# A gated MLP on one Trainium2 core: the last column group's gate by seven block products, and a down-projection that begins in the middle

## The chip, the cores and the metric

The kernel runs as one program on one core of a Trainium2 chip. The core has a matrix engine (TensorE; PE in the profile, its weight loads PEld), a vector engine (VectorE, DVE), a scalar engine (ScalarE, ACT), GpSimd (POOL) and a sync engine (SyncE, SP), which here only issues DMA transfers. Matmuls read SBUF and write PSUM banks of 128 x 512 numbers. The metric is the device time of one execution in microseconds.

## The reference, cut to what matters

Two layers of a decoder trunk work on 512 tokens of 1024 features: layer 0 has attention and a short convolution as its mixer, layer 1 a gated linear attention. Behind each mixer stands the gated MLP that the change touches, and behind that a small gated embedding:

```python
def _conv_ffn(h, w_up, conv_w, conv_b, w_down):
    u = _causal_depthwise_conv(h @ w_up, conv_w) + conv_b
    gate, up = jnp.split(u, 2, axis=-1)
    return (jax.nn.gelu(gate, approximate=False) * up) @ w_down

# in each layer i:
    x = x + _conv_ffn(_rms_norm(x, ffn_norm[i]), ffn_w_up[i], ffn_conv_w[i], ffn_conv_b[i], ffn_w_down[i])
```

`w_up` is 1024 x 5632: 2816 gate columns and 2816 value columns. `w_down` is 2816 x 1024. The convolution is causal, of width 3 along the tokens, with own weights for every column.

## The kernel before

Activations are kept with features on the 128 partitions and tokens along the row, so a tile is 128 features x 512 tokens. Everything is float32, done as three matmuls: each operand is split into a high part (ScalarE, rounded to the matmul's format) and a low part (VectorE, the rest), and a product is high x high, high x low and low x high (`mm3`, L153 to L160; `split`, L97). Weights are loaded 1024 x 256 numbers at a time into one of two `raw` buffers (8 KB a partition, 1 MB in all) and cut into high and low pieces `wh` and `wl` (`cut`, L119 to L139), of which three of each fit, a piece being 128 x 1024.

The MLP (`ffn`, L871) goes over its 2816 = 11 x 256 gate columns in 11 groups d = 0 to 10. A group makes two gate column tiles and two value column tiles, applies the three taps to each (`taps`, L883: one ScalarE pass and two VectorE passes), a Gelu to the gates, and multiplies gate and value (L1018). The product is two activations, numbers f = 2d and 2d + 1; there are 22. Groups come in two kinds:

- Plain groups (the `else` branch at L988): each of the four column tiles is 8 x 3 matmuls, 128 x 128 weights by 512 tokens. Weights are asked for under `high_priority(offset=300)`.
- Seven-product groups, `SEVEN = (4, 10)`, so d = 4 to 9 (L970): the gate's 1024 x 256 weights and the 512 tokens are taken as 2 x 2 blocks, and their product is formed from seven block products in place of eight, after the scheme of Strassen and Winograd (`seven`, L827). A block product is 4 x 3 matmuls of 256 tokens. VectorE forms the weights' sums for it (`seven_forms`, L813), and the tokens' sums are made once (`sums`, L771; list `forms`). The group's values stay plain, 48 matmuls of 512 tokens. The order of TensorE is written out by hand here (`manual_schedule(engines={ET.PE})`): the first steps of group d + 1 (18 + 12 + 6 matmuls, `begin`, L957) stand at the end of group d, and `prepare(d + 1)` (L950) loads and cuts its weights.

Buffers tie the parts together. The tag `four` has seven tiles of 128 x 4 x 512: five hold finished products (`kept`, four activations each), and the others take split activations, two activations with both parts in a tile. The tags `b0` and `b1` have eight tiles each: they hold the tokens' sums (`forms`) as long as seven-product groups run, and then split activations, one in a pair. The tag `zt` has two, so a group's gate and value tiles follow those of the group before.

When the last seven-product group (d = 9) is traced, activations 0 to 7 are split into `b` pairs (L1021); after the loop 8 to 21 are split into `four` tiles (L1026). The down-projection (`project`, L350) takes two of the eight output column tiles at a time, and for these three blocks of inputs: activations 0 to 7, 8 to 15 and 16 to 21, with a load and a cut for each. A block is 2 x 8 x 3 = 48 matmuls of 512 tokens (the last 36).

Other than where it is written out by hand, the order of each engine's list is set when the program is built, by a planner that takes the instructions in the order of the code as their priority, moves an instruction ahead by the given number of places under `high_priority`, and lets one start when its inputs and a free buffer are there. On the chip each engine then works its list in that order.

```python
                    with tc.high_priority(offset=300):
                        wg = self.weights(wu[:, :, gates(d)], ND, 256)
                        wv = self.weights(wu[:, :, values(d)], ND, 256)
```

Of the kernel before, what the change touches and what calls it, by code (L numbers as in the profile page):

```python
# [18 lines left out]
P = 128  # L19
# [3 lines left out]
ND = D // P  # L23
DFF = 2816
NF = DFF // P
# [3 lines left out]
ET = mybir.EngineType  # L29
LEVELS = (64, 32, 16, 8, 4, 2, 1)  # L30
CW = 512
SEVEN = (4, 10)
TWO_PI = 2.0 * np.pi
PI_SAFE = 3.1415925

# [22 lines left out]
class Kernel:  # L58
# [288 lines left out]
        nc.scalar.copy(R, pr)  # L347
        return R

    def project(self, load, ks, n_out, done):  # L350

        nk = len(ks)
        for m2 in range(0, n_out, 2):
            pss = [self.ps(), self.ps()]
            for k0 in range(0, nk, 8):
                kn = min(8, nk - k0)
                raw = self.raw(kn, 2 * P)
                load(raw, k0, slice(m2 * P, (m2 + 2) * P))
                w = self.cut(raw, "b")
                for c in range(2):  # L360
                    for k in range(kn):
                        self.mm3(
                            pss[c], w(k, c * P, (c + 1) * P), ks[k0 + k],
                            start=k0 + k == 0, stop=k0 + k == nk - 1,
                        )
            for c in range(2):
                done(m2 + c, pss[c])
# [503 lines left out]
    def ffn(self, i, next_gain):  # L871
        nc, a, tc = self.nc, self.a, self.tc
# [2 lines left out]
        wu = a["ffn_w_up"][i].rearrange("(k p) n -> p k n", p=P)  # L875
        w0, w1, w2, bb = self.fcv
        with tc.tile_pool(name=f"ffn{i}", bufs=1) as fp:
            forms, kept, acts = [], [], []

            def both():  # L880
                return fp.tile([P, 2, S], F32, tag="zt", name=self.nm("zt"), bufs=2)

            def taps(y, ps, f, more=None, normed=True):  # L883
                z = ps
                if more is not None:
                    z = fp.tile([P, S + 2], F32, tag="z", name=self.nm("z"), bufs=3)[:, :S]
                    h2 = lambda x: x.rearrange("p (u t) -> p u t", u=2)
                    nc.vector.tensor_tensor(
                        h2(z), h2(ps), more.unsqueeze(1).to_broadcast([P, 2, S // 2]), ALU.add
                    )  # L890
                elif not normed:
                    z = fp.tile([P, S + 2], F32, tag="z", name=self.nm("z"), bufs=3)[:, :S]
                    nc.vector.tensor_tensor(z, ps, R, ALU.mult)
                nc.scalar.activation(y, z, AF.Identity, scale=w2[:, f : f + 1], bias=bb[:, f : f + 1])  # L894
                for tap, w in ((1, w1), (2, w0)):
                    nc.vector.scalar_tensor_tensor(  # L896
                        out=y[:, tap:], in0=z[:, : S - tap], scalar=w[:, f : f + 1], in1=y[:, tap:],
                        op0=ALU.mult, op1=ALU.add,
                    )

            def columns(w, c, bank):
                ps = bank()
                for k in range(ND):
                    self.mm3(ps, w(k, c * P, (c + 1) * P), xg[k], start=k == 0, stop=k == ND - 1)
                return ps
# [10 lines left out]
            def place(d):  # L916

                if d == NF // 2 - 1:
                    return None
                if d % 2 == 0:  # L920
                    kept.append(self.four(fp, F32))
                return kept[d // 2][:, 2 * (d % 2) : 2 * (d % 2) + 2]

            def split_pair(x):
                four = self.four(fp)
                self.split((four[:, :2], four[:, 2:]), x)
                acts.extend([(four[:, u], four[:, 2 + u]) for u in range(2)])

            def at(f):
                return kept[f // 4][:, f % 4]  # L930

            def gates(d):
                return slice(256 * d, 256 * d + 256)

            def values(d):
                return slice(DFF + 256 * d, DFF + 256 * d + 256)

            def normed(scratch):

                out = []  # L940
                for m in range(ND):
                    out.append(self.pair(self.fp, "a0", "a1"))
                    self.split(out[m], scratch[m // 2][:, m % 2])
                return out

            def value(w, ps, k0, k1):
                for k in range(k0, k1):
                    self.mm3(ps, w(k, 0, P), xg[k], start=k == 0, stop=k == ND - 1)

            def prepare(d):  # L950

                rg, rv = loaded(d)
                w1 = column(rv, 1)
                ws = self.seven_forms(rg)
                return self.seven(rg, ws, xg, forms), w1, column(rv, 0)

            def begin(d, steps, w):  # L957

                ps = self.pa()
                value(w, ps, 0, 6)  # L960
                next(steps)
                value(w, ps, 6, ND)
                return lambda y: taps(y[:, 1], ps, NF + 2 * d + 1)

            first, last = SEVEN
            scratch = [self.four(fp, F32) for _ in range(ND // 2)]
            late = None
            for d in range(NF // 2):
                g, y = both(), both()
                if first <= d < last:  # L970
                    with tc.manual_schedule(engines={ET.PE}):
                        next(steps)
                        V0 = self.pa()
                        value(w0c, V0, 0, ND // 2)
                        next(steps)
                        value(w0c, V0, ND // 2, ND)
                        X, Y, more = next(steps)
                        mine = late

                        if d + 1 < last:  # L980
                            steps, w1c, w0c = prepare(d + 1)
                            late = begin(d + 1, steps, w1c)
                        mine(y)
                        taps(y[:, 0], V0, NF + 2 * d)
                        taps(g[:, 0], X, 2 * d)
                        taps(g[:, 1], Y, 2 * d + 1, more)
                        nc.scalar.activation(g, g, AF.Gelu)
                else:  # L988
# [4 lines that stand above are left out]
                    todo = []  # L993
                    for c in range(2):
                        pss = [columns(w, c, self.ps) for w in (wg, wv)]
                        if R is None:
                            R = self.spread()

                        def finish(c=c, pss=pss):
                            taps(g[:, c], pss[0], 2 * d + c, None, d > first)  # L1000
                            nc.scalar.activation(g[:, c], g[:, c], AF.Gelu)
                            taps(y[:, c], pss[1], NF + 2 * d + c, None, d > first)

                        if d == first - 1:
                            todo.append(finish)
                        else:
                            finish()
                    if d == first - 1:
                        xg = normed(scratch)
                        with tc.manual_schedule(engines={ET.PE}):  # L1010
                            steps, w1c, w0c = prepare(first)
                            late = begin(first, steps, w1c)
                        for f in todo:
                            f()
                u = place(d)
                if u is None:
                    u = y
                nc.vector.tensor_tensor(u, g, y, ALU.mult)  # L1018
                for j in {0: (0, 1), 1: (2, 3)}.get(d, ()):
                    forms.append(self.sums(j, gain, R, scratch[j]))  # L1020
                if d == last - 1:  # L1021
                    for f in range(8):
                        hl = self.pair(self.fp, "b0", "b1")
                        self.split(hl, at(f))
                        acts.append(hl)
            for d in range(4, NF // 2):  # L1026
                split_pair(y if d == NF // 2 - 1 else kept[d // 2][:, 2 * (d % 2) : 2 * (d % 2) + 2])
            self.begin_norm(("a0", "a1"))
            done = self.residual(next_gain)
            if i == 1:  # L1030
# [12 lines left out]
                    nc.vector.tensor_tensor(self.xT[m], self.xT[m], ps, ALU.add)  # L1043
                    self.blocks(m, next_gain, half)

            self.project(self.rows(a["ffn_w_down"][i]), acts, ND, done)
            if i == 0:
                self.end_norm()
            else:
# [704 lines left out]
```

## Time and profile before

| | us |
|---|---|
| median of 3 runs (1239.39 to 1239.8) | 1239.51 |
| the profiled execution | 1240.1 |
| its span, first to last instruction | 1238.3 |
| TensorE busy | 1227.8 |
| VectorE busy | 847.8 |
| ScalarE busy | 604.6 |
| GpSimd busy | 43.6 |

The profile is of one execution, whose own time is 1.8 us longer than the span of its instructions and 0.6 us above the median. A row of a group of instructions reads: line, engine, operation, output<-inputs with shapes, count | busy time, mean duration in ns | idle time of the engine before them and what ended it. In a table of stretches each row gives a stretch in microseconds from the span's start, its length, and the busy time of each engine with its instruction count, then the granted clock of TensorE (1.00 is full), the DMA share and the GB/s. In order of time a row gives start, duration, engine, line, operation, output<-inputs, shapes, count and, in brackets, the idle time before it. Matmuls are pipelined, so the pace of a series is read from its starts, not its durations.

### The profile page before, as it was taken

To read this page: it belongs to the slowest core of one execution; us is meant where nothing else is said; L and a number is where in the kernel's file an instruction comes from. 1 tells how busy PE (TensorE), PEld (TensorE's weight loads), DVE (VectorE), ACT (ScalarE), POOL (GpSimd) and SP (SyncE) were. 2 spreads that over 40 slices of the span, in tenths; PEclk is the share of its full clock that TensorE was granted. 3 is DMA by queue.
4 is the path that set the end of the run, shared out by engine and by line. 5 is a ranking of instruction groups with operands and counts; after the bars stand their busy time and mean duration, and the time that the engine had idled before them with its cause. 6 is when DMAs were issued, how large, how long until landed. Compare 5 with 4: busy or idle time off the path is not lost.

```text
span 1238.3 us, 16087 instructions
## 1 busy us (share of the span) xinstructions
PE 1227.8 (99%) x6416; PEld 1036.6 (84%) x6416; DVE 847.8 (68%) x1323; ACT 604.6 (49%) x963; POOL 43.6 (4%) x64
## 2 busy tenths in 40 slices
PE   9999999999999999999999999999999999999998
PEld 8877788889899888888987888888889998888887
DVE  6886556987778833346679875549977779544495
ACT  7466333555557522234563554435455558333374
POOL 2500000000000000000100000000000000000000
PEclk9999999999999999999999999999999999999999
DMA  7221332323233332223322222332332324222411
GB/s 215 86 88 51 88 103 69 102 69 124 81 109 111 109 99 94 94 80 99 111 91 68 69 69 68 102 98 83 101 108 71 129 77 137 94 94 94 152 44 69
DMA packets 111007, 117.50 MB, mean 95 GB/s; under 512 B 2728, under 2 KB 106210, under 8 KB 110932
## 3 DMA queue, kind: packets, MB, share of 16 engines
q1 hardware_dynamic: 109568, 115.35, 28.7%
q8 instruction: 50, 0.82, 0.3%
q0 software_dynamic: 560, 0.42, 0.3%
q10 hardware_dynamic: 804, 0.70, 0.2%
q14 instruction: 25, 0.20, 0.1%
HBM read 114.37 MB, written 2.10 MB: 94 GB/s over the span
## 4 chain that ended last, share of the span: by engine, by line
PE 88%; DVE 7%; ACT 2%; issue 2%; POOL 1%; DMA 0%; ACTq 0%; DVEq 0%; POOLq 0%
PE ps L158 19%; PE ps L159 19%; PE ps L160 19%; PE pa L159 4%; PE pa L158 4%; PE pa L160 4%; PE ps L844 2%; PE ps L843 2%; PE ps L842 2%; DVE wl L139 1%; PE ps L1168 1%; PE ps L1166 1%; PE ps L1167 1%; PE pa L844 1%; PE pa L843 1%
## 5 line engine op out<-in xcount | busy, mean ns | idle before, releaser
L138 ACT ACTIVATE wh<-raw 128x1024 fp32r<-128x1024 f32 (+4 forms) x188 | 188.4, 1004 | 324.6 <-PE ps L159 272.7
L139 DVE TENSOR_TENSOR wl<-raw,wh 128x1024 fp32r<-128x1024 f32 (+4 forms) x188 | 216.8, 1155 | 179.8 <-ACT wh L138 179.5
L158 PE MATMUL ps<-a,wh 128*128 128x512 f32 x480 | 187.6, 391 | 0.0
L159 PE MATMUL ps<-a,wh 128*128 128x512 f32 x480 | 187.2, 390 | 0.0
L160 PE MATMUL ps<-a,wl 128*128 128x512 f32 x480 | 186.9, 389 | 0.0
L158 PE MATMUL ps<-b,wh 128*128 128x512 f32 x320 | 126.0, 395 | 0.6 <-ACT b L102 0.5
L160 PE MATMUL ps<-b,wl 128*128 128x512 f32 x320 | 125.7, 393 | 0.0
L159 PE MATMUL ps<-b,wh 128*128 128x512 f32 x320 | 124.9, 391 | 0.0
L158 PEld LDWEIGHTS ps<-a,wh 128*128 128x128 f32 x480 | 90.2, 188 | 18.9 <-issue 0.7
L160 PEld LDWEIGHTS ps<-a,wl 128*128 128x128 f32 x480 | 90.1, 188 | 18.9
L159 PEld LDWEIGHTS ps<-a,wh 128*128 128x128 f32 x480 | 90.2, 188 | 18.7 <-issue 0.3
L158 PE MATMUL ps<-four,wh 128*128 128x512 f32 x224 | 87.1, 389 | 0.0
L159 PE MATMUL ps<-four,wh 128*128 128x512 f32 x224 | 87.1, 389 | 0.0
L160 PE MATMUL ps<-four,wl 128*128 128x512 f32 x224 | 87.1, 389 | 0.0
L158 PE MATMUL pa<-a,wh 128*128 128x512 f32 x192 | 75.3, 392 | 0.0
L159 PE MATMUL pa<-a,wh 128*128 128x512 f32 x192 | 75.3, 392 | 0.0
L160 PE MATMUL pa<-a,wl 128*128 128x512 f32 x192 | 74.7, 389 | 0.0
L158 PEld LDWEIGHTS ps<-b,wh 128*128 128x128 f32 x320 | 60.0, 188 | 14.2 <-ACT b L102 1.3
L159 PEld LDWEIGHTS ps<-b,wh 128*128 128x128 f32 x320 | 60.1, 188 | 12.5
L160 PEld LDWEIGHTS ps<-b,wl 128*128 128x128 f32 x320 | 60.1, 188 | 12.5
L896 DVE SCALAR_TENSOR_TENSOR zt<-z,vfa,zt 128x511 f32<-128x511 f32 (+1 forms) x88 | 64.0, 745 | 5.3 <-ACT zt L894 5.0
L807 ACT ACTIVATE wh<-raw 128x1024 fp32r<-128x1024 f32 x36 | 38.0, 1057 | 37.0 <-DVE raw L820 20.1
(423 smaller groups left out, 2509.3 us busy)
## 6 DMA issues: line engine op xcount, KB each, us to landing
raw<-in_ffn_w_up_dram SPq DMA_DIRECT2D x44, 1024.0 KB, 5.0
raw<-in_ffn_w_down_dram SPq DMA_DIRECT2D x16, 1024.0 KB, 5.0
raw<-in_hy_w_in_dram SPq DMA_DIRECT2D x8, 1024.0 KB, 5.1
raw<-in_gla_w_in_dram SPq DMA_DIRECT2D x8, 1024.0 KB, 5.2
raw<-in_ffn_w_down_dram SPq DMA_DIRECT2D x8, 768.0 KB, 4.5
raw<-in_ple_w_gate_dram SPq DMA_DIRECT2D x6, 1024.0 KB, 5.0
raw<-in_gla_w_out_dram SPq DMA_DIRECT2D x4, 1024.0 KB, 5.1
raw<-in_gla_w_in_dram SPq DMA_DIRECT2D x4, 672.0 KB, 4.1
```

Of the source, the lines that this page charges most:

```text
L138: nc.scalar.activation(hv, v, AF.Copy)
L139: nc.vector.tensor_tensor(lv, v, hv.bitcast(F32), ALU.subtract)
L158: mm(out, lh, rh, start=start, stop=False)
L159: mm(out, lh, rl, start=False, stop=False)
L160: mm(out, ll, rh, start=False, stop=stop)
L807: nc.scalar.activation(h, src, AF.Copy)
L842: mm(out, wh, xh, start=first and j == 0, stop=False, **kw)
L843: mm(out, wh, xl, start=False, stop=False, **kw)
L844: mm(out, wl, xh, start=False, stop=j == ND // 2 - 1, **kw)
L896: nc.vector.scalar_tensor_tensor(out=y[:, tap:], in0=z[:, : S - tap], scalar=w[:, f : f + 1], in1=y[:, tap:], op0=ALU.mult, op1=ALU.add,)
L1166: mm(o, lh, rh, start=first and j == 0, stop=False, **kw)
L1167: mm(o, lh, rl, start=False, stop=False, **kw)
```

## The change

The last group, d = 10, becomes a seven-product group as well: `SEVEN = (4, 11)`. It is the last of that kind, so nothing is prepared behind its products; in that place the code now has `split_acts()`, which splits the finished activations 0 to 19 in a new order: 8 to 13 into `four` tiles, 0 to 3 into `b` pairs, 14 and 15, then 4 to 7 and 16 to 19. The split of 0 to 7 behind d = 9 and the loop behind all groups go; 20 and 21 are split when d = 10 is done. The list of activations is filled by number, not by appending.

`project` gets an argument `first`. For the first pair of output columns, the MLP's down-projection takes the block of activations 8 to 15 first, then 0 to 7, then 16 to 21, and its three loads and cuts are traced under `high_priority(offset=300)`. The later column pairs keep the old order. All other calls of `project`, and the later pairs, trace their loads under an offset of zero. The first and last matmul of an accumulation are marked by the new order of the blocks.

```diff
-SEVEN = (4, 10)
+SEVEN = (4, 11)
...
-    def project(self, load, ks, n_out, done):
+    def project(self, load, ks, n_out, done, first=()):
...
-            for k0 in range(0, nk, 8):
+            lead = [k0 for k0 in first if m2 == 0]
+            k0s = lead + [k0 for k0 in range(0, nk, 8) if k0 not in lead]
+            for k0 in k0s:
                 kn = min(8, nk - k0)
-                raw = self.raw(kn, 2 * P)
-                load(raw, k0, slice(m2 * P, (m2 + 2) * P))
-                w = self.cut(raw, "b")
+                with self.tc.high_priority(offset=300 if lead else 0):
+                    raw = self.raw(kn, 2 * P)
+                    load(raw, k0, slice(m2 * P, (m2 + 2) * P))
+                    w = self.cut(raw, "b")
                 for c in range(2):
                     for k in range(kn):
                         self.mm3(
                             pss[c], w(k, c * P, (c + 1) * P), ks[k0 + k],
-                            start=k0 + k == 0, stop=k0 + k == nk - 1,
+                            start=k0 == k0s[0] and k == 0, stop=k0 == k0s[-1] and k == kn - 1,
                         )
...
-            forms, kept, acts = [], [], []
+            forms, kept, acts = [], [], [None] * NF
...
-            def split_pair(x):
+            def split_pair(f, x=None):
+                if x is None:
+                    x = kept[f // 4][:, f % 4 : f % 4 + 2]
                 four = self.four(fp)
                 self.split((four[:, :2], four[:, 2:]), x)
-                acts.extend([(four[:, u], four[:, 2 + u]) for u in range(2)])
-
-            def at(f):
-                return kept[f // 4][:, f % 4]
+                acts[f : f + 2] = [(four[:, u], four[:, 2 + u]) for u in range(2)]
+
+            def split_kept(t):
+                for f in range(4 * t, 4 * t + 4):
+                    acts[f] = self.pair(self.fp, "b0", "b1")
+                    self.split(acts[f], kept[t][:, f % 4])
+
+            def split_acts():
+                for f in (8, 10, 12):
+                    split_pair(f)
+                split_kept(0)
+                split_pair(14)
+                split_kept(1)
+                for f in (16, 18):
+                    split_pair(f)
...
                         if d + 1 < last:
                             steps, w1c, w0c = prepare(d + 1)
                             late = begin(d + 1, steps, w1c)
+                        else:
+                            split_acts()
                         mine(y)
...
-                if d == last - 1:
-                    for f in range(8):
-                        hl = self.pair(self.fp, "b0", "b1")
-                        self.split(hl, at(f))
-                        acts.append(hl)
-            for d in range(4, NF // 2):
-                split_pair(y if d == NF // 2 - 1 else kept[d // 2][:, 2 * (d % 2) : 2 * (d % 2) + 2])
+            split_pair(NF - 2, y)
...
-            self.project(self.rows(a["ffn_w_down"][i]), acts, ND, done)
+            self.project(self.rows(a["ffn_w_down"][i]), acts, ND, done, first=(8,))
```

## The prediction

> **What bounds the kernel now.** I read the page first, then the waits of TensorE, then a table of stretches around the place of the change, then single instructions in order of time. The page:
>
> ```profile
> span 1238.3 us, 16087 instructions
> PE 1227.8 (99%) x6416; PEld 1036.6 (84%) x6416; DVE 847.8 (68%) x1323; ACT 604.6 (49%) x963; POOL 43.6 (4%) x64
> PEclk9999999999999999999999999999999999999999
> ...
> PE 88%; DVE 7%; ACT 2%; issue 2%; POOL 1%; DMA 0%; ACTq 0%; DVEq 0%; POOLq 0%
> ...
> raw<-in_ffn_w_up_dram SPq DMA_DIRECT2D x44, 1024.0 KB, 5.0
> ```
>
> See three things. TensorE is busy for 99% of the span at full granted clock, the chain that ended last is 88% TensorE, and a weight block lands 5.0 us after its issue. The busy share alone doesn't prove that matmuls follow each other without a hole, so the stretches come next: in each layer the last seven-product group (d = 9), the plain last group (d = 10), and the first two rows of the down-projection.
>
> ```profile
> core 0: us, PE busy (x) PEld busy (x) DVE busy (x) ACT busy (x) POOL busy (x), PEclk, DMA share, GB/s
> 378.03:399.06 21.03, 21.03 (x134) 19.07 (x133) 19.83 (x26) 16.36 (x24) 0.00 (x0) 1.00 0.31 101
> 399.06:420.85 21.79, 21.79 (x98) 18.04 (x97) 21.53 (x27) 14.49 (x20) 0.00 (x0) 1.00 0.30 97
> 420.85:450.77 29.92, 29.92 (x133) 24.77 (x132) 12.34 (x13) 8.67 (x10) 0.00 (x0) 1.00 0.31 101
> 1016.74:1037.78 21.04, 21.04 (x134) 19.08 (x133) 19.82 (x26) 16.37 (x24) 0.00 (x0) 1.00 0.31 100
> 1037.78:1059.57 21.79, 21.79 (x98) 18.03 (x97) 21.53 (x27) 14.48 (x20) 0.00 (x0) 1.00 0.30 97
> ```
>
> The columns are the stretch, its length, and each engine's busy time and instructions. TensorE is busy through all of each stretch (the count takes in two matmuls that overlap its edge: 132 and 96 by the code). So here the time is the sum of the paces of matmuls, and any hole would be new. VectorE is nearly as full as TensorE in the plain group (21.53 of 21.79 us) and has room only behind it (12.34 of 29.92 us).
>
> **The change, part by part.** *Fewer matmul columns.* The pace is read from starts, since matmuls overlap:
>
> ```profile
> 267.65 0.39 PE L159 MATMUL ps<-a,wh 128*128 128x512 f32 x1
> ...
> 276.72 0.39 PE L160 MATMUL pa<-a,wl 128*128 128x512 f32 x1
> 276.94 0.28 PE L842 MATMUL pa<-a,wh 128*128 128x256 f32 x1
> ...
> 278.25 0.28 PE L844 MATMUL pa<-a,wl 128*128 128x256 f32 x1
> ```
>
> From the first to the 41st of the wide ones: 9.07 / 40 = 0.227 us each. From the first to the 12th of the narrow ones: 1.31 / 11 = 0.119 us. A plain gate is 2 columns x 8 k x 3 = 48 wide matmuls, 10.88 us; seven products are 7 x 4 x 3 = 84 narrow ones, 10.00 us. That would be 0.88 us; the whole groups in the table differ by less, 21.79 - 21.04 = 0.75 us, because wide matmuls that follow narrow ones run a little slower. I take 0.75, since it holds all of that; two layers give **-1.50 us**. The bounds of this term are -1.50 and -1.76.
>
> The Trainium skill, "TensorE: Matmul & The Clock Gate", section "Wait — 56ns, not 53.3ns?", gives the pace as columns over 2.4 GHz and about 2.5 ns for each matmul. An estimate by it is 48 x 215.8 - 84 x 109.2 = 1.19 us a layer, -2.4 us in all. The rows above have some 13 ns over the columns' time on either width, five times that, and the 36 additional matmuls of a layer pay it; the trace decides.
>
> *What the seven form adds on VectorE and ScalarE.* Durations of the pieces:
>
> ```profile
> L139 DVE TENSOR_TENSOR wl<-raw,wh 128x1024 fp32r<-128x1024 f32 x152 | 185.6, 1223 | 114.5 <-ACT wh L138 114.1
> L896 DVE SCALAR_TENSOR_TENSOR zt<-z,vfa,zt 128x511 f32<-128x511 f32 x44 | 32.4, 746 | 5.0 <-ACT zt L894 5.0
> L1018 DVE TENSOR_TENSOR four<-zt,zt 128x1024 f32<-128x1024 f32 x20 | 24.4, 1220 | 0.1
> L103 DVE TENSOR_TENSOR b<-four,b 128x512 fp32r<-128x512 f32 x32 | 21.4, 684 | 0.0
> L103 DVE TENSOR_TENSOR four<-four,four 128x1024 fp32r<-128x1024 f32 x12 | 14.4, 1216 | 0.0
> L102 ACT ACTIVATE four<-four 128x1024 fp32r<-128x1024 f32 x12 | 12.4, 1052 | 2.2 <-DVE four L103 2.2
> L807 ACT ACTIVATE t<-raw 128x512 fp32r<-128x512 f32 x12 | 7.6, 637 | 0.2 <-DVE raw L822 0.2
> 386.60 0.37 ACT L858 COPY more<-pa 128x256 f32<-128x256 f32 x1 [0.54 <-PE pa L844]
> ```
>
> A plain group cuts four weight pieces, 4 x 1.22 = 4.9 us of VectorE. A seven group cuts five and a half-size one, subtracts four half-size blocks and adds one partial sum: 5 x 1.22 + 6 x 0.68 = 10.2 us (all of the six are 512 elements wide, as the b split is). So 5.3 us more for VectorE, and about 1.05 + 0.64 + 5 x 0.37 = 3.5 us for ScalarE (a cut, a half-size one, five half-bank copies). Its cover is the down-projection's first stretch, where VectorE is free for 29.92 - 12.34 = 17.6 us; on the path it costs nothing as long as the splits meet their two dates, worked out below.
>
> *The date of the first activations.* The down-projection now starts on activations 8 to 15. The old d = 9 group is the model for the new d = 10 group, since it too prepares no seven-product successor; moved on by one period of 21.04 us, its rows give the new times:
>
> ```profile
> 387.34 3.34 SPq L112 DMA_DIRECT2D raw<-in_ffn_w_up_dram  x2
> 390.20 1.22 DVE L1018 TENSOR_TENSOR four<-zt,zt 128x1024 f32<-128x1024 f32 x1
> 391.33 1.29 DVE L103 TENSOR_TENSOR b<-four,b 128x512 fp32r<-128x512 f32 x2
> 392.55 0.75 DVE L896 SCALAR_TENSOR_TENSOR zt<-pa,vfa,zt 128x511 f32<-128x511 f32 x1
> 393.21 0.68 DVE L103 TENSOR_TENSOR b<-four,b 128x512 fp32r<-128x512 f32 x1
> 393.81 0.74 DVE L896 SCALAR_TENSOR_TENSOR zt<-pa,vfa,zt 128x510 f32<-128x510 f32 x1
> 394.47 0.68 DVE L103 TENSOR_TENSOR b<-four,b 128x512 fp32r<-128x512 f32 x1
> 395.07 1.22 DVE L139 TENSOR_TENSOR wl<-raw,wh 128x1024 fp32r<-128x1024 f32 x1
> 396.20 2.35 DVE L103 TENSOR_TENSOR four<-four,four 128x1024 fp32r<-128x1024 f32 x2
> 398.48 1.22 DVE L139 TENSOR_TENSOR wl<-raw,wh 128x1024 fp32r<-128x1024 f32 x1
> ```
>
> The old d = 9 group ends where the table's second stretch begins, at 399.07; before that VectorE had already split four activations into b pairs and two pairs into fours, and cut the first two weight pieces. The new one ends at 420.1. Its d = 9 product (L1018) starts at 390.20 + 21.04 = 411.2. From there the list is that product 1.22, four fours (8 to 15) 4 x 1.22, four b pairs (0 to 3, which free the buffer for 14 and 15) 4 x 0.68, and the two weight cuts 2.44: 11.3 us, done at 422.5. Activation 14 is read by the 19th matmul of the down-projection, 420.1 + 18 x 0.227 = 424.2. That leaves 1.7 us. If the two taps of the late value column (2 x 0.75) stay ahead, as they were in d = 9, 0.2 us are left; against that, two of the seven fours buffers are free from the start, so 8 to 11 need not wait for 411.2. I take no stall. The bounds are nothing and 4.6 us a layer, worked out with the rivals.
>
> *The date of the last activations.* After 422.5 VectorE has four b pairs (4 to 7) 2.7, two fours (16 to 19) 2.4, eight taps 8 x 0.75 with one sum 0.7, the product 1.2, the split of 20 and 21 1.2, and four weight cuts 4 x 1.22 at most: 19.1 us, done at 441.6. The third block (activations 16 to 21) starts two blocks of 48 wide matmuls after 420.1, at 441.9, and reads activation 20 after 12 more, at 444.6. The cover is 3.0 us; each microsecond beyond it would be paid twice, once a layer.
>
> *Loads and weights.* The rows of SP: the plain weights were asked for at 387.34, 11.7 us ahead of their first matmul, and the first piece was cut at 395.07 + 1.22 = 396.3, 2.8 us ahead. The down-projection's first three blocks now get the same lead of 300 places, the numbers of loads stay (two for d = 10, three for the first columns), and they use the same two raw buffers. SP only issues loads, and d = 10's own pair now goes one period earlier, as d = 9's did without a hole. Cost nothing; bound without that cover 5.0 + 1.05 + 1.22 = 7.3 us a layer.
>
> *The rest.* Block order and the start and stop flags leave the 144 matmuls of a column pair as they are. The other projections get a lead of zero places; no row can show that this moves nothing, so I bound it by the longest wait of TensorE in the second mixer, which a shuffled order might repeat or take away:
>
> ```profile
> PE pa L1434 <- DVE F L1432: 1.5, 2, 1.0
> ```
>
> That is up to 1.0 us either way; I take zero, since that part of the program is untouched.
>
> Sum: the profiled execution took 1240.1 us (span 1238.3 and 1.8 around it) and should become 1240.1 - 1.5 = 1238.6. The median of the runs shown, 1239.51, lies 0.6 below it, so I predict 1239.5 - 1.5 = **1238.0 us**.
>
> **The rivals.** *First activations late* (the one that ends slower). Place: the first block of the down-projection. If VectorE began the splits only after the last product, act 8 would be ready 1.05 + 1.22 = 2.3 us after it and act 14 after 1.05 + 4 x 1.22 + 4 x 0.68 = 8.7 us, against a date of 4.1: 4.6 us a layer, 2 x 4.6 - 1.5 = +7.7, 1247 us. From 2.0 us a layer on (act 14 later than 6.1 us after the last product) it makes the kernel slower by over 0.2%. For it: a VectorE that is busy for 19.83 + 21.53 = 41.4 of 42.8 us. Against it: the splits at 391.33 and 396.20 ran inside a seven group. VectorE works its list in order, so a tap that waits for a bank would hold the splits behind it; the Trainium skill's same page, in its table of specifications, calls that queue strict FIFO, which no row here contradicts.
>
> *A short stall.* The same place or act 20, by 0.3 to 2.0 us a layer: 1238.6 to 1242.0, within 0.2%, about what a measurement of this kernel can tell from no change (2.5 us). For it: margins of 0.2 to 3.0 us.
>
> *A down-projection load takes a raw buffer ahead of d = 10's own weights.* Then TensorE waits a whole load and cut, 7.3 us a layer, 2 x 7.3 - 1.5 = +13.1, 1253 us. The 300 places reach back beyond the point where d = 10 is prepared. Against it: the plain weights had the same lead, and their load at 387.34 came a period after this row:
>
> ```profile
> 366.30 3.33 SPq L910 DMA_DIRECT2D raw<-in_ffn_w_up_dram  x2
> ```
>
> *The matmuls save something else.* If a matmul cost its columns alone, the 48 x 512 - 84 x 256 = 3072 columns fewer would be worth (0.227 - 0.119) / 256 = 0.42 ns each, 1.3 us a layer: 1236.9. If the narrow ones ate the gain, so that the change doesn't do what it says, 1239.5. The 0.75 us of whole groups speaks against both. The Trainium skill's rule for the pace, weighed above, stands near the first.
>
> **How the numbers follow.** No hole, 1238.0 (its own range 1237.0 to 1239.0: the 1.0 us of the mixers either way): 0.66. Short stall: 0.12. First activations late: 0.12. Load late: 0.05. Matmuls at their columns' cost: 0.02; no gain of the matmuls: 0.02; an unseen wait that goes, with over 2.5 us: 0.01. The range of 1237.0 to 1242.0 holds the first two and the sixth, 0.80. Faster by over 0.2%: 0.03; within: 0.80; slower: 0.17.
>
> **What would show it.** In the trace after: 168 more narrow matmuls and 96 fewer wide ones; a last group of 21.04 us in both layers; the first matmul of the down-projection on a four, 0.12 us behind the last narrow one; no wait of TensorE between the first seven group and the end of the down-projection. A wait of L158 on L103 (four) at its 1st, 7th, 13th or 19th matmul would show the first rival, one on L139 the third, one in the third block late last activations. The prediction is wrong if any hole over 2.0 us a layer stands there.

## The result and the profile after

The changed kernel takes 1237.99 us (median of 22 runs), the kernel before beside it 1239.83 (22 runs): a ratio of 0.9986 with a 95% interval of 0.9979 to 0.9992. That is 1.84 us less, and by the interval between 1.0 and 2.6 us less. One of the 22 runs of the changed kernel took 4132.6 us, for a reason that no profile here shows; the ratio and its interval leave it out. The profiled execution after took 1237.57 us, with a span of 1235.8.

The page of the kernel after, the lines that answer to those shown of before:

```profile
span 1235.8 us, 16256 instructions
PE 1225.1 (99%) x6488; PEld 1037.8 (84%) x6488; DVE 857.8 (69%) x1337; ACT 611.8 (50%) x975; POOL 44.2 (4%) x64
...
PEclk9999999999999999999999999999999999999999
...
PE 88%; DVE 7%; ACT 2%; issue 2%; POOL 1%; DMA 0%; SPq 0%; DVEq 0%; ACTq 0%; POOLq 0%
```

TensorE has 72 instructions more: 168 narrow matmuls more and 96 wide ones fewer. VectorE has 10.0 us more work and ScalarE 7.2, which is 5.0 and 3.6 a layer, and the chain that ended last is TensorE to the same 88%. So more work was done on two engines and a little less on the one that bounds the kernel.

The table of stretches of the kernel after (columns as in the prediction): in layer 0 the group d = 9, the group d = 10 and the down-projection's first stretch, then d = 10 of layer 1.

```profile
377.27:398.31 21.04, 21.04 (x135) 19.08 (x133) 19.38 (x24) 14.16 (x19) 0.00 (x0) 1.00 0.31 101
398.31:419.35 21.04, 21.04 (x135) 19.08 (x133) 19.69 (x26) 15.56 (x24) 0.00 (x0) 1.00 0.31 100
419.35:449.27 29.92, 29.92 (x134) 24.78 (x133) 19.44 (x23) 13.28 (x16) 0.00 (x0) 1.00 0.31 101
...
1035.94:1056.98 21.04, 21.04 (x134) 19.08 (x133) 19.57 (x26) 15.56 (x24) 0.00 (x0) 1.00 0.31 101
```

The last group is now 21.04 us long instead of 21.79, TensorE is busy through all of it, and VectorE's work in the down-projection's first stretch went from 12.34 to 19.44 us without lengthening that stretch by a hundredth.

Spans of single executions also differ where nothing was changed, so I measure every kernel below between the same two matmuls of a layer: the first one of the MLP's norm (on `ones` and `acc`) and the last one of the down-projection that reads `wh`. TensorE in order of time, first before, then after; the 615.14 and 613.35 rows are one matmul of the second mixer.

```profile
188.00 0.26 PE L324 MATMUL pa<-ones,acc 128*128 128x1 f32 x1
...
540.09 0.39 PE L159 MATMUL ps<-four,wh 128*128 128x512 f32 x1
...
615.14 0.51 PE L158 MATMUL ps<-b,wh 128*128 128x512 f32 x1 [0.17 <-ACT vt L1329]
...
826.69 0.26 PE L324 MATMUL pa<-ones,acc 128*128 128x1 f32 x1
...
1178.80 0.39 PE L159 MATMUL ps<-four,wh 128*128 128x512 f32 x1
```

```profile
187.24 0.26 PE L324 MATMUL pa<-ones,acc 128*128 128x1 f32 x1
...
419.23 0.28 PE L848 MATMUL ps<-a,wl 128*128 128x256 f32 x1
419.35 0.40 PE L158 MATMUL ps<-four,wh 128*128 128x512 f32 x1
...
423.46 0.39 PE L158 MATMUL ps<-four,wh 128*128 128x512 f32 x1
...
443.86 0.39 PE L158 MATMUL ps<-four,wh 128*128 128x512 f32 x1
...
538.60 0.39 PE L159 MATMUL ps<-four,wh 128*128 128x512 f32 x1
...
613.35 0.51 PE L158 MATMUL ps<-b,wh 128*128 128x512 f32 x1
...
824.88 0.26 PE L324 MATMUL pa<-ones,acc 128*128 128x1 f32 x1
...
1176.23 0.39 PE L159 MATMUL ps<-four,wh 128*128 128x512 f32 x1
```

Before: 540.09 - 188.00 = 352.09 and 1178.80 - 826.69 = 352.11. After: 351.36 and 351.35. The two MLPs are shorter by 0.73 and 0.76, together 1.49 us. The spans differ by 2.5, and most of the rest, 0.76 us, lies ahead of the first MLP (188.00 against 187.24), where both kernels issue the same instructions in the same order. So of the 1.84 us between the medians 1.49 are found in the changed part, and the other 0.35, which the interval of 1.0 to 2.6 doesn't tell from zero, I attribute to nothing. Among the kernels below, what lies outside the two stretches varies by some 1.5 us from one profiled execution to another, so I take stretches from the profile and totals from medians.

### The profile page after: what moved, and what is told of

Its sections match the earlier page's. It is cut to its first block, busy times and chain, and to the rows that moved or that the text cites. A ratio compares the mean times of both kernels' runs of the same rounds, so it can differ in the third digit from the quotient of the medians.

```text
span 1235.8 us, 16256 instructions
## 1 busy us (share of the span) xinstructions
PE 1225.1 (99%) x6488; PEld 1037.8 (84%) x6488; DVE 857.8 (69%) x1337; ACT 611.8 (50%) x975; POOL 44.2 (4%) x64
## 4 chain that ended last, share of the span: by engine, by line
PE 88%; DVE 7%; ACT 2%; issue 2%; POOL 1%; DMA 0%; SPq 0%; DVEq 0%; ACTq 0%; POOLq 0%
PE ps L158 18%; PE ps L159 18%; PE ps L160 18%; PE pa L159 5%; PE pa L158 5%; PE pa L160 5%; PE ps L848 3%; PE ps L847 3%; PE ps L846 3%; DVE wl L139 1%; PE pa L848 1%; PE pa L847 1%; PE pa L846 1%; PE ps L1181 1%; PE ps L1179 1%
## 5 line engine op out<-in xcount | busy, mean ns | idle before, releaser
L138 ACT ACTIVATE wh<-raw 128x1024 fp32r<-128x1024 f32 (+4 forms) x184 | 184.3, 1003 | 312.3 <-PE ps L159 258.5
L139 DVE TENSOR_TENSOR wl<-raw,wh 128x1024 fp32r<-128x1024 f32 (+4 forms) x184 | 212.0, 1153 | 166.3 <-ACT wh L138 165.9
L158 PE MATMUL ps<-a,wh 128*128 128x512 f32 x416 | 162.7, 391 | 0.0
L159 PE MATMUL ps<-a,wh 128*128 128x512 f32 x416 | 162.3, 390 | 0.0
L160 PE MATMUL ps<-a,wl 128*128 128x512 f32 x416 | 162.0, 390 | 0.0
L158 PEld LDWEIGHTS ps<-a,wh 128*128 128x128 f32 x416 | 78.1, 188 | 16.6 <-issue 0.7
L159 PEld LDWEIGHTS ps<-a,wh 128*128 128x128 f32 x416 | 78.2, 188 | 16.3 <-issue 0.3
L160 PEld LDWEIGHTS ps<-a,wl 128*128 128x128 f32 x416 | 78.1, 188 | 16.2
L158 PE MATMUL pa<-a,wh 128*128 128x512 f32 x224 | 87.8, 392 | 0.0
L159 PE MATMUL pa<-a,wh 128*128 128x512 f32 x224 | 87.8, 392 | 0.0
L160 PE MATMUL pa<-a,wl 128*128 128x512 f32 x224 | 87.1, 389 | 0.0
L900 DVE SCALAR_TENSOR_TENSOR zt<-z,vfa,zt 128x511 f32<-128x511 f32 (+1 forms) x92 | 66.9, 744 | 5.9 <-ACT zt L898 5.4
L811 ACT ACTIVATE wh<-raw 128x1024 fp32r<-128x1024 f32 x42 | 44.4, 1057 | 41.1 <-DVE raw L824 22.1
```

The source lines that it names most:

```text
L138: nc.scalar.activation(hv, v, AF.Copy)
L139: nc.vector.tensor_tensor(lv, v, hv.bitcast(F32), ALU.subtract)
L158: mm(out, lh, rh, start=start, stop=False)
L159: mm(out, lh, rl, start=False, stop=False)
L160: mm(out, ll, rh, start=False, stop=stop)
L811: nc.scalar.activation(h, src, AF.Copy)
```

## The experiments

My theory was the prediction's: seven products in place of eight are worth 0.75 us of TensorE in each group and layer, and everything else in the change only has to arrive on time. The rivals were that some of the gain comes from the new order of the splits and blocks or from the lead of the loads, that the splits are close to their date, or that the matmul term is another size. "Stretches" are the two differences of layer 0 and 1 against before, as above. Times are compared with runs of the kernel before on the same chip (medians 1239.77, 1239.91 and 1239.73 in the three series).

**Which part gives the gain: the seven products alone.** The kernel before with one constant changed; splits, blocks and lead stay the old ones.

```diff
-SEVEN = (4, 10)
+SEVEN = (4, 11)
```

> Seven products for the last group with nothing else: the down-projection starts on activations 0 to 7 without a lead, and four of their b pairs come free only when the last product has read the sums. The matmul account with ample cover: 1.5 us under before. The rival, that the new order and lead are what keeps TensorE fed: a hole of 2 to 5 us a layer ahead of the down-projection, so 2.5 to 8.5 us over before.

Measured: 1237.80 us (1237.21 to 1237.99), ratio 0.9984 (0.9975 to 0.9993); stretches -0.74 and -0.74. The table of stretches of this kernel, the last group of both layers:

```profile
398.78:419.82 21.04, 21.04 (x134) 19.08 (x133) 19.75 (x26) 15.52 (x24) 0.00 (x0) 1.00 0.31 100
1036.29:1057.33 21.04, 21.04 (x134) 19.08 (x133) 19.91 (x26) 15.52 (x24) 0.00 (x0) 1.00 0.32 101
```

No hole in either, and the same 21.04 us. The constant gives the whole gain; the new order and the lead add nothing that can be measured.

**The change without the lead.** The kernel after, its down-projection loads traced like all others.

```diff
-                with self.tc.high_priority(offset=300 if lead else 0):
+                with self.tc.high_priority(offset=0):
```

> The changed kernel without the lead of 300 places for the first three blocks; block order and splits as changed. If the planner would place loads and cuts early anyhow, because buffers are free: like the changed kernel, 1.5 us under before. If the lead matters: the first cut comes behind the splits and taps, a hole of 1 to 5 us a layer, so 0.5 to 8.5 us over before.

Measured: 1238.02 us (1237.55 to 1238.55), ratio 0.9986 (0.9977 to 0.9995); stretches -0.73 and -0.75. The lead is worth nothing here.

**The new order alone (with the lead).** The kernel after with the old range of seven-product groups; since activations 18 and 19 don't exist yet when the splits are traced, their split moves behind the loop.

```diff
-SEVEN = (4, 11)
+SEVEN = (4, 10)
...
-                for f in (16, 18):
-                    split_pair(f)
+                split_pair(16)
...
+            split_pair(18)
             split_pair(NF - 2, y)
```

> The order alone: the last group stays plain, but the activations are split in the new order and the down-projection starts on 8 to 15 with the lead of 300 places. The matmul account (all of the gain is 0.75 us a layer of matmul pace): as before, 0.0 us, within 0.4 us, and no wait of TensorE. The new start (the gain comes from the earlier loads and the other block order): at least half of the 1.8 us of the medians, so 0.9 us or more under the kernel before.

Measured: 1241.01 us (1240.26 to 1242.00), ratio 1.0010 (1.0001 to 1.0019); stretches +0.67 and +0.65. Neither theory foresaw a loss. TensorE's waits of this kernel name it; the columns are the total, how often, and the longest:

```profile
PE ps L158 <- DVE zt L900: 0.8, 2, 0.4
```

The place in layer 0, TensorE in order of time:

```profile
409.72 0.39 PE L160 MATMUL ps<-a,wl 128*128 128x512 f32 x1
410.51 0.47 PE L158 MATMUL ps<-a,wh 128*128 128x512 f32 x1 [0.40 <-DVE zt L900]
```

and VectorE ahead of it:

```profile
401.72 1.22 DVE L103 TENSOR_TENSOR four<-four,four 128x1024 fp32r<-128x1024 f32 x1
402.86 1.29 DVE L103 TENSOR_TENSOR b<-four,b 128x512 fp32r<-128x512 f32 x2
...
404.72 1.22 DVE L103 TENSOR_TENSOR four<-four,four 128x1024 fp32r<-128x1024 f32 x1
...
409.62 0.74 DVE L900 SCALAR_TENSOR_TENSOR zt<-ps,vfa,zt 128x510 f32<-128x510 f32 x1
```

The two starts stand 0.79 us apart instead of 0.227. My reading: the splits, traced ahead of d = 9's taps, run ahead of them on VectorE (401.72 to 405.9), so the last tap that reads a PSUM bank ends at 410.36, and the plain group's next column must wait for that bank.

**The same with the splits traced behind the taps.** To test that reading I moved the call, and nothing else.

```diff
-                        else:
-                            split_acts()
                         mine(y)
                         taps(y[:, 0], V0, NF + 2 * d)
                         taps(g[:, 0], X, 2 * d)
                         taps(g[:, 1], Y, 2 * d + 1, more)
                         nc.scalar.activation(g, g, AF.Gelu)
+                        if d + 1 == last:
+                            split_acts()
```

> The order alone (last group plain), but the splits are traced behind the taps of group 9. If the 0.6 us a layer that the order alone lost is a PSUM bank that the taps free late because the splits stand ahead of them: the wait on L900 goes, 0.0 us against before, within 0.4 us. If the new block order itself costs it: 1.2 us over before, as with the splits ahead.

Measured: 1240.09 us (1239.23 to 1240.39), ratio 1.0001 (0.9992 to 1.0010); stretches -0.01 and -0.01. VectorE of this kernel:

```profile
402.99 0.74 DVE L900 SCALAR_TENSOR_TENSOR zt<-ps,vfa,zt 128x510 f32<-128x510 f32 x1
```

The same tap, the last one that reads a PSUM bank, now ends at 402.99 + 0.74 = 403.7, 6.6 us earlier; the wait is gone, and so is the loss. In the new order, then, the splits' place ahead of the taps costs 0.66 us a layer as long as a plain group follows. When d = 10 is a seven-product group nothing plain follows, and that cost disappears.

**How much cover the splits have.** The kernel after, with VectorE's part of the splits of activations 8 to 15 done twice (4 x 1.22 = 4.9 us more) and four times (14.6 us more); the repeats write the same numbers again.

```diff
-    def split(self, hl, src, gain=None):
+    def split(self, hl, src, gain=None, times=1):
...
-            nc.vector.tensor_tensor(l, src, h.bitcast(F32), ALU.subtract)
+            for _ in range(times):
+                nc.vector.tensor_tensor(l, src, h.bitcast(F32), ALU.subtract)
...
-                self.split((four[:, :2], four[:, 2:]), x)
+                self.split((four[:, :2], four[:, 2:]), x, times=2 if 8 <= f < 16 else 1)
```

> The changed kernel with VectorE's part of the splits of activations 8 to 15 done twice: 4 x 1.22 = 4.9 us more for VectorE ahead of the down-projection. In the changed kernel's trace the last of them ends at 417.8 and TensorE reads it at 423.4, 5.6 us of cover. By that cover: 1.5 us under before, no hole, or under 0.5 us a layer. By the cover of 1.7 us that the prediction worked out: a hole of some 3 us a layer, 4 to 5 us over before.

Twice: 1238.02 us (1237.15 to 1238.71), ratio 0.9983 (0.9974 to 0.9992); stretches -0.73 and -0.77. No hole, so the cover is more than the 1.7 us that I had worked out. The last repeat of the split of 14 and 15, on VectorE:

```profile
420.93 1.22 DVE L104 TENSOR_TENSOR four<-four,four 128x1024 fp32r<-128x1024 f32 x1
```

> The same four times: 14.6 us more for VectorE ahead of the down-projection. By a cover of 5.6 us: 14.6 - 5.6 = 9.0 us of hole a layer, less up to 3 us where taps give way and TensorE takes what is ready, so 10 to 17 us over before. By the prediction's 1.7 us: some 13 us a layer, 24 us over before. If those dates don't bind, because VectorE has room elsewhere: under 2 us over before.

Four times: 1252.06 us (1250.40 to 1253.31), ratio 1.0091 (1.0075 to 1.0106); stretches +7.22 and +6.28, that is 8.0 and 7.0 us a layer more than the kernel after. In the records of both these kernels the line numbers of splits and matmuls are one higher. Its waits of TensorE:

```profile
PE ps L160 <- DVE four L104: 9.6, 4, 3.3
```

So the holes make 4.8 us a layer, and the rest of the loss must be elsewhere. TensorE around the longer hole of layer 0, and three stretches there:

```profile
429.73 0.39 PE L159 MATMUL ps<-four,wh 128*128 128x512 f32 x1
433.44 0.80 PE L160 MATMUL ps<-four,wh 128*128 128x512 f32 x1 [3.33 <-DVE four L104]
...
434.46 0.63 PE L159 MATMUL ps<-four,wh 128*128 128x512 f32 x1
434.89 0.63 PE L160 MATMUL ps<-four,wh 128*128 128x512 f32 x1
```

```profile
425.20:433.50 8.30, 3.50 (x15) 2.23 (x13) 8.30 (x11) 1.20 (x3) 0.00 (x0) 0.92 0.00 0
433.50:438.70 5.20, 5.20 (x12) 4.07 (x13) 5.20 (x7) 2.94 (x3) 0.00 (x0) 0.50 0.01 3
438.70:445.00 6.30, 6.30 (x29) 5.20 (x28) 5.31 (x9) 2.00 (x3) 0.00 (x0) 0.98 0.47 166
```

Behind the hole of 3.33 us matmuls start 0.427 us apart, at a granted clock of 0.50, for 5.2 us; a dozen matmuls at 0.2 us too much are 2.4 us. With 4.8 us of holes and the slower restart of a matmul or two behind each, that is most of the 8.0 of layer 0; in layer 1 the slow phase is shorter (shown in the last section). The prediction's first rival is real, then, but it needs splits far longer than they are.

**The matmul term in the other direction: five seven-product groups.** The kernel before with one constant changed.

```diff
-SEVEN = (4, 10)
+SEVEN = (4, 9)
```

> The kernel before with one seven-product group fewer (d = 4 to 8). The matmul account: 0.75 us a layer lost, 1.5 us over before, no hole. By columns alone (1.3 us a layer): 2.6 us over before. By the new-start rival the number of groups matters little: under 0.5 us.

Measured: 1243.12 us (1242.93 to 1243.63), ratio 1.0028 (1.0017 to 1.0040); stretches +0.72 and +2.10. Layer 0 pays the term. Layer 1 pays 1.4 us more. Against the same matmuls of layer 0 it falls back at the value weights of three groups in a row: 0.2 us at 955.1, 0.4 at 976.5 and 0.8 at 998.3, the last for d = 8. TensorE, SP and ScalarE of this kernel at the last of the three:

```profile
998.34 0.50 PE L160 MATMUL pa<-a,wl 128*128 128x512 f32 x1 [0.53 <-DVE wl L139]
```

```profile
986.76 2.16 SPq L910 DMA_DIRECT2D raw<-in_ffn_w_up_dram  x2
```

```profile
995.96 1.06 ACT L138 ACTIVATE wh<-raw 128x1024 fp32r<-128x1024 f32 x1 [3.79 <-DMA raw<-in_ffn_w_up_dram]
```

and SP and ScalarE of the kernel before at the same load:

```profile
983.98 3.33 SPq L910 DMA_DIRECT2D raw<-in_ffn_w_up_dram  x2
```

```profile
992.08 1.06 ACT L138 ACTIVATE wh<-raw 128x1024 fp32r<-128x1024 f32 x1 [1.38 <-DMA raw<-in_ffn_w_up_dram]
```

An SP row of two issues runs from the first to the end of the second, an issue being 0.37 us. Here the two loads of 1 MB stand 2.16 - 0.37 = 1.8 us apart, and ScalarE's first cut of the second one starts 995.96 - 988.55 = 7.4 us behind its issue. Before they stood 3.0 us apart, and that took 992.08 - 986.94 = 5.1 us.

**More of the same: seven-product groups from d = 3 on.** First on the kernel before, then on the kernel after.

```diff
-SEVEN = (4, 10)
+SEVEN = (3, 11)
```

> Seven products for groups 3 to 10 in the code of before (no new order, no lead). The matmul account: two more groups a layer than before, 4 x 0.75 = 3.0 us under before, 1.5 us under seven products alone. The rival: the normed activations, prepared for group 4 so far, are now due a group earlier, while VectorE still makes the sums; then a hole of 1 to 4 us a layer at the first seven-product group, so between 1 us under and 5 us over before.

```diff
-SEVEN = (4, 11)
+SEVEN = (3, 11)
```

> The same groups 3 to 10 in the changed kernel. If order and lead are worth nothing, the same time as the version without them, within 0.4 us; if they matter once VectorE is fuller, up to 1 us less.

Measured on the kernel before: 1241.88 us (1240.16 to 1243.99), ratio 1.0015 (1.0006 to 1.0024), stretches -0.50 and +1.84. On the kernel after: 1242.25 us (1239.73 to 1242.89), ratio 1.0014 (1.0006 to 1.0023), stretches -0.49 and +2.42. Two more groups should give each layer about -1.5, so on the kernel before 1.0 us is lost in layer 0 and 3.3 in layer 1. Single executions of it spread over 3.8 us, and the profiled one, 1240.16, is the fastest. TensorE's waits on the kernel before with this constant, where the kernel before has none in its MLPs:

```profile
PE pa L160 <- DVE wl L139: 0.8, 2, 0.5
PE ps L844 <- DVE t L808: 0.7, 2, 0.3
```

The starts that came over 0.15 us late add up to 0.7 us in layer 0 and 2.4 in layer 1. Of these 3.1 us, 2.2 stand at the four waits for cut weights in the rows above; for the other starts the profile names no wait, and the rest of the loss is spread over many small ones. So further groups gained nothing here, and weights that come late are the largest part of the loss that the trace shows; what makes up the rest stays open.

**Values loaded first.** If the late load is the second of a pair, swapping the two should move the delay away from the value weights. On the kernel with groups from 3 on, on the one with groups 4 to 10, and on the one with five groups:

```diff
-                for raw, cols in zip(out, (gates(d), values(d))):
+                for raw, cols in zip(out, (values(d), gates(d))):
...
-                return out
+                return out[::-1]
```

> Groups 3 to 10 in the code of before, and of the two loads of a seven-product group the values' first, which TensorE needs first. If the holes of groups 3 to 10 come from the value weights that land late: the waits on L139 go (2.7 us of the 3.3 us lost in layer 1, 0.3 us in layer 0), those on the piece t2 of the first group stay (0.6 us a layer); 4 x 0.75 - 1.2 = 1.8 us under before. If they come from a VectorE that is too full: as without the swap, 2 us over before.

> Seven products for groups 4 to 10 alone, with the values' load first. No hole stood there without the swap, so by either account the same time as without it: 1.5 to 2.0 us under before.

> Groups 4 to 8 in the code of before, with the values' load first. If the 1.3 us lost in layer 1 by the version without the swap came from value weights that land late: that goes, and what stays is the matmul term of 1.5 us, with up to 0.7 us of the mixer: 1.5 to 2.2 us over before. If not: 3.3 us over before, as without it.

Measured: from 3 on, 1239.05 us (1237.37 to 1239.94), ratio 0.9993 (0.9985 to 1.0002), stretches -0.17 and +0.90 in a profiled execution of 1239.94, the slowest of its kernel; groups 4 to 10, 1238.21 us (1237.48 to 1238.96), ratio 0.9987 (0.9978 to 0.9996), stretches -0.65 and -0.69; five groups, 1242.19 us (1240.86 to 1243.95), ratio 1.0020 (1.0011 to 1.0029), stretches +0.75 and +0.74 in a profiled execution of 1240.86. TensorE's wait in the first of these:

```profile
PE ps L844 <- DVE t L808: 1.8, 5, 0.5
```

The waits at the value weights are gone, but now the blocks of the gate's weights come late, and the gain of two more groups isn't reached. With five groups the late starts of layer 1 are gone in the profiled execution, which supports the reading of the load; that execution is the fastest of its kernel, though, and why its median is 1.3 us higher stays open. With groups 4 to 10 the swap gives nothing, since there is no hole to close. No version tried is faster than the changed kernel by more than the intervals.

## Why the prediction was right, step by step

**The time.** Predicted 1238.0 us, measured 1237.99; the case that it named, no hole, is what the trace shows: TensorE has no wait between the norm and the end of the down-projection in either layer. The agreement to a hundredth is luck: 1.50 of the drop were predicted, the stretches gave 1.49, and the medians 1.84.

**The matmul term** was predicted as 0.75 us a layer from the difference of whole groups. The change gave 0.73 and 0.76, the constant alone 0.74 and 0.74, and one group fewer cost 0.72 in the layer where nothing came late. That the size shows in both directions makes it the best established number here. The bound from the paces alone (0.88) was too high, and the rival of columns alone (1.3) is out. The Trainium skill ("TensorE: Matmul & The Clock Gate", "Wait — 56ns, not 53.3ns?") led to an estimate of 1.19; the measured 0.74 is against it, as the starts in the trace of before already were.

**What the seven form adds** was predicted as 5.3 us of VectorE and 3.5 of ScalarE a layer; the page shows 5.0 and 3.6, and the stretches show that they cost nothing.

**The dates of the activations** are where the sizes were off, on the safe side. VectorE of the kernel after:

```profile
390.57 2.35 DVE L103 TENSOR_TENSOR four<-four,four 128x1024 fp32r<-128x1024 f32 x2
...
394.28 1.21 DVE L103 TENSOR_TENSOR four<-four,four 128x1024 fp32r<-128x1024 f32 x1
...
415.46 1.22 DVE L139 TENSOR_TENSOR wl<-raw,wh 128x1024 fp32r<-128x1024 f32 x1
416.59 1.22 DVE L103 TENSOR_TENSOR four<-four,four 128x1024 fp32r<-128x1024 f32 x1
...
434.43 1.23 DVE L103 TENSOR_TENSOR four<-zt,four 128x1024 fp32r<-128x1024 f32 x1 [1.13 <-ACT four L102]
```

14 and 15 were ready at 416.59 + 1.22 = 417.8 and 14 was read at 423.46 (shown above): a cover of 5.6 us where I had 1.7. 20 and 21 were ready at 435.7 and 20 was read at 443.86: 8.2 us where I had 3.0. The step that was mis-sized is the list of the first date: it put all four splits of 8 to 15 behind d = 9's product, and I noted the two free `four` buffers only as a reason that 8 to 11 need not wait. In the trace three of the four, 8 to 13, ran a whole group earlier (390.57 and 394.28). Behind d = 9's product there were then only four `b` splits, two taps, one weight cut and the split of 14 and 15; the second weight cut came after it. The doubled splits bear this out from the other side: the last one ends at 420.93 + 1.22 = 422.2, 1.8 us ahead of the matmul that reads it there (423.96), and holes open only somewhere between 4.9 and 14.6 us more. So the chances of 0.12 each for late activations and for a short stall were too high for this order.

**Loads and weights** were predicted at no cost by the example of the plain group. SP of the kernel after:

```profile
386.57 3.34 SPq L914 DMA_DIRECT2D raw<-in_ffn_w_up_dram  x2
407.62 0.37 SPq L375 DMA_DIRECT2D raw<-in_ffn_w_down_dram  x1
```

d = 10's own pair is issued ahead of the down-projection's, so the raw buffer was not taken out of turn, and 407.62 is 11.7 us ahead of the first matmul that uses it, as predicted. The first piece was cut by 416.7, 2.7 us ahead. (One reading of the rows of before was not right: the cut of the second piece, at 398.48 + 1.22 = 399.70, ended 0.6 us behind that group and not ahead of its end; the sum doesn't use it.) The cost of nothing was right; that the lead is the reason was not, since without it the time is the same.

**The zero offset elsewhere** was given up to 1.0 us either way. Outside the ends of the two MLPs each engine's instructions stand in the same order as before, so the planner moved nothing there. Of TensorE's waits in the second mixer one differs by more than 0.03 us, the matmul at 615.14 (0.17 us of waiting before, none after). Counted from the end of the first MLP it came between 0.36 us sooner and 0.71 us later across the profiled kernels, so I don't count it to this change.

**What the prediction didn't ask** is which part of the change carries the term. It summed the parts as one, and the runs took them apart: the constant is worth -1.5 us, the lead 0, and the new order +1.3 on its own and 0 together with the constant.

## What to carry to other kernels

Where the bounding engine has no hole, a saving on it is read from the difference of two whole groups that are already in the trace, and the work it adds elsewhere is free up to a date that has to be worked out; list what each buffer lets start early, since that list decides the margin. Try the smallest edit by itself: here one constant held all of the gain, and the reordering that came with it was worth nothing together with the constant and a loss without it. A term that repeats per group is not an offer for more groups: with d = 3 added no layer got faster than with groups 4 to 10, and the waits that the trace names were for weights that came too late.

## What the runs showed of the hardware that was not expected

A hole of 3.33 us on TensorE cost more than itself, in both layers of the kernel with the splits done four times. In layer 0 the granted clock behind it was 0.50 for 5.2 us, and matmuls started 0.427 us apart instead of 0.227. In layer 1 a hole of the same length was followed by 1.3 us at nearly full clock (0.98), and only then by 3.4 us at about half:

```profile
1080.70:1084.10 3.40, 3.40 (x10) 2.67 (x8) 3.40 (x5) 1.86 (x2) 0.00 (x0) 0.51 0.00 0
```

The shorter hole just before, 4.8 - 3.33 = 1.5 us, was not followed by this in either layer. The Trainium skill, "TensorE: Matmul & The Clock Gate", "Part 1: The HAM clock gate", has the clock halve after an idle window of about 3.4 us and return after about as much busy time; the trace agrees with the size of the step and nearly with the idle time (3.33 us), and its slow phase was longer in layer 0 (5.2 us) and as long in layer 1 (3.4 us). What sets the start and the length of the slow phase these two holes don't show.

Of two loads of 1 MB the second took 5.1 us to the first cut when issued 3.0 us behind the first, and 7.4 us when issued 1.8 us behind. The distance alone doesn't set it: in layer 1 of the kernel with five groups a second load was issued 3.62 - 0.37 = 3.25 us behind the first, at 946.05, and its first cut came 952.70 - 946.05 = 6.65 us later.

```profile
942.80 3.62 SPq L910 DMA_DIRECT2D raw<-in_ffn_w_up_dram  x2
...
952.70 1.06 ACT L138 ACTIVATE wh<-raw 128x1024 fp32r<-128x1024 f32 x1 [3.19 <-DMA raw<-in_ffn_w_up_dram]
```

What else delayed that load stays open. The Trainium skill, "DMA: Bandwidth & Descriptors", "Issuing engines are not separate DMA queues", says of DMAs that they run on the same 16 DMA engines and interleave, whichever engine started them, which fits; no run here measured the sharing by itself.
